# S5's output operands loaded ahead, a gate tile moved behind cross attention, and two moves at the feed-forward half's start and end

## The chip, the cores and the metric

The kernel runs on one NeuronCore of one Trainium2 chip. Its five engines each work through a queue of their own, in order: TensorE (PE, matrix products), VectorE (DVE), ScalarE (ACT), GpSimd (POOL), and SyncE (SP), which here issues the DMA transfers. The metric is the device time in microseconds (us); 0.2% of it is 3.3 us.

## The reference

One encoder layer, without masks, for two sequences of 512 tokens and 1024 channels, in float32, followed by a last RMS norm. The two sequences have weights in common, so the kernel handles them as one batch of 1024 columns.

```python
xn = rmsnorm(x, norm_mix);  mn = rmsnorm(mem, norm_mem)
u, q, k, v, xq, g = split(xn @ w_in)
y_s5   = z * sigmoid(z @ w_glu + b_glu)     # z = gelu(S5 scan both ways of u + d*u)
y_diff = differential attention of rope(q), rope(k), v
y_x    = cross attention of xq over 256 memory rows (mk, mv from mn @ w_mem_kv)
merged = sum over n of sigmoid(g[n]) * (branch[n] @ w_up[n])
x = x + merged @ w_out
gate, up = split(rmsnorm(x, norm_ffn) @ w_ffn_in)
x = x + (silu(gate) * up) @ w_ffn_out
y = rmsnorm(x, norm_final)
```

## The kernel before

**Products.** A float32 product is made of three: each operand is split into a rounded high part and the low rest (`split`: ACT casts the high part, L128, DVE subtracts for the low one, L129), and PE does high x high, low x high and high x low (L61). Tiles have 128 rows, 512 columns go through at a time; `xh, xl` are the halves of the normed input, `wh, wl` those of a weight tile, which arrives as `wf` (L140). A tile of `w_in` takes 48 such matmuls, 24 for each sequence.

**What sets the order.** The kernel's program is written in stages, and PE's order of work within a stage is mixed by hand: `queue` is a list of generators, `fill(n)` takes about n matmuls out of it, between the steps of the work that has waits. Gate tiles (`gate_units`: 48 matmuls, a tanh on ACT, a store to `gD` at L376) are what is mostly drawn on. The table `NG` says how many gate tiles each of three stages may use; its last number is for the stage from S5's output to the product with `w_glu`. Except where `PE.on` fixes PE's order, the framework orders the instructions of each engine by its own estimate of when they can start. Room in SBUF comes in named pools with a number of slots (`open_tags`); a new tile waits for the last user of the slot that it gets.

**S5's output (L1495 to L1524).** Convolution kernels of the 32 channel groups (`gD5`, in DRAM) and state outputs (`cD`) have been prepared. Four output groups follow, o = 0 to 3, each of 8 channel groups. A group loads `c_r` and `c_n` (L1502, L1503, 576 KB each) and its kernels `w_` in eight pieces (L1506), then PE does for each channel group three products, with `w_`, `c_r` and `c_n` in this order (L1517 to L1519), ACT copies the result to `y_` (L1520), and SP stores it in eight pieces (L1522). One tag `ow` with six slots holds all three operands of two groups, and the loads of a group are written behind the stores of the one before. Between the groups, PE does gate tiles.

**Cross attention.** 32 steps (4 heads, 2 sequences, 4 row blocks): scores, softmax, a `fill(5)`, two transposes of `e` (L64), the split of those into `xpTh`, `xpTl`, another `fill(5)`, and every four steps six matmuls with the memory's values (`bkoo`). The queue behind it ends with the first tile of the differential attention's queries, `units(w_in[4])`, whose result DVE turns with rope tables (L685, L687).

**The first feed-forward half.** `out_tile` makes x1 = x + merged @ w_out (L899 adds), 8 tiles of rows; the last four output tiles, for rows 3 and 7, are interleaved. `operands(i)` norms tiles i and i + 4, makes four sums of quadrants (`quad_sums`: DVE L907, L909, L910, POOL L908) and splits all seven operands into `th`, `tl`. The half's 22 weight tiles (KFF) each hold gate and up weights, 2 x 2 blocks; a Winograd scheme needs seven products for what plain blocks do in eight, 84 matmuls a tile. For it `weights4(i)` splits the blocks A11, A12, A22 and makes four sums S1 to S4 on POOL (L954 to L957, tile `ws`), which are split too, into the pool `aps`. DVE combines the products (L1035), norms (L1087), and makes the activation `ac` (L1090, L1091), with a tanh on ACT (L1088) and a product on POOL (L1089); `ac` goes to DRAM as `aD`. `rs` and `acc` are the norm's factors, for which PE does a few small products (`onec`, `ident`).

**Its end.** The second half needs the activations back in pairs: `act_pair(p)` loads `fa` and `fb` (L1054, L1055) and makes quad sums `ts`. The first two pairs are loaded and summed early, while the last tiles still run, and split (`pairs`) when the loop is done.

The tag `ld`, with four slots of 512 KB, is used by loads of many stages, `fa` and `fb` among them; `ws` had two slots of its own.

Of the kernel before, what the change touches and what calls it, by code (L numbers as in the profile page):

```python
# [37 lines left out]

NPREP = (16, 27)

NG = (7, 5, 7)
ROUND = 12582912.0


# [23 lines left out]
def encoder(ctx: ExitStack, tc: tile.TileContext, a, out):  # L68
# [547 lines left out]
    for _ in xq_units(0):  # L616
        pass
    xq = {h: xq_units(h) for h in range(1, 4)}
    queue += [xq[1], gate_units(), xq[2], xq[3], v_units(0, v0), units(a["w_in"][4], xh, xl, dq0.__setitem__)]
    PE.on = True  # L620
    steps = [(h, s, lt) for h in range(4) for s in range(NS) for lt in range(4)]
    es, pT = {}, {}
# [1 line left out]
    for i in range(-AHEAD, len(steps) + 1):  # L624
        if i + AHEAD < len(steps):
            h, s, lt = steps[i + AHEAD]
            if h and s == lt == 0:
                finish(xq[h])
            ms = slice(s * NMEM, (s + 1) * NMEM)
            qh, ql = (q_[:, lt * P : (lt + 1) * P] for q_ in qs[h, s])  # L630
            sc = bank("sc")
            PE.matmul(sc[:, :NMEM], qh, mkh[h][:, ms], start=True, stop=False)
            PE.matmul(sc[:, :NMEM], qh, mkl[h][:, ms], start=False, stop=False)
            PE.matmul(sc[:, :NMEM], ql, mkh[h][:, ms], start=False, stop=True)
            e, r = softmax_parts(xa, xcol, sc[:, :NMEM], NMEM, P ** -0.5, "x", bufs=3)
# [12 lines left out]
        fill(5)  # L648
        if i > 0 and steps[i - 1][2] == 3:
            h, s, _ = steps[i - 1]  # L650
            pTh, pTl = pT.pop((h, s))
            oo = bank("oo")
            hs = slice(h * P, (h + 1) * P)
            for j in range(2):
                PE.matmul(oo, mvh[s][:, j, hs], pTh[:, j, :], start=(j == 0), stop=False)
                PE.matmul(oo, mvh[s][:, j, hs], pTl[:, j, :], start=False, stop=False)
                PE.matmul(oo, mvl[s][:, j, hs], pTh[:, j, :], start=False, stop=(j == 1))
            osb = xa.tile([P, L], F32, tag="osb", name="xosb", bufs=1)
            S.copy(osb, oo)
            nc.sync.dma_start(bD[2, h, :, s * L : (s + 1) * L], osb)  # L660
        half_piece(last_e)
# [221 lines left out]
    ves.close()  # L883
    tes = ExitStack()
    open_tags(tes, side="right", th0=2, tl0=2)
    ses = ExitStack()
    open_tags(ses, side="right", x1=4, xr=2, ts=1)
    x1D = drp.tile([KD, P, NT], F32, name="x1D")
# [24 lines left out]
    def quad_room(i):  # L913
        j = i // 2 % 2
        return slot(f"th{j}", [P, 7, L], F32R, "th"), slot(f"tl{j}", [P, 7, L], F32R, "tl")

    def quad_split(i, xa_, xb_, t_):

        th, tl = quad_room(i)
        split(th[:, 0], tl[:, 0], xa_[:, 0:L])  # L920
        split(th[:, 1:3].rearrange("p a n -> p (a n)"), tl[:, 1:3].rearrange("p a n -> p (a n)"), xb_)
        split(th[:, 3:5], tl[:, 3:5], t_[:, 0:2])
        split(th[:, 5:7], tl[:, 5:7], t_[:, 2:4])
        return th, tl

    def operands(i):
# [8 lines left out]
    def weights4(i):  # L935

        nonlocal last_w
        a1, a2 = (wp.tile([P, DM], F32, tag="wf", name="wf") for _ in range(2))
        nc.sync.dma_start(a1, a["w_fg"][i])
        last_w = nc.sync.dma_start(a2, a["w_fu"][i])  # L940
        res = {}

        def sp(pool, src, sfx, *names):
            n = len(names) * H
            wh, wl = (pool.tile([P, DM], F32R, tag=t_ + sfx, name=t_, bufs=2) for t_ in ("wh", "wl"))
            split(wh[:, :n], wl[:, :n], src)
            for j, nm in enumerate(names):
                res[nm] = (wh[:, j * H : (j + 1) * H], wl[:, j * H : (j + 1) * H])

        sp(wp, a1, "", "A11", "A12")  # L950
        sp(wp, a2[:, H:], "", "A22")
        yield res
        s12, s34 = (slot("ws", name="ws") for _ in range(2))
        PO.tensor_tensor(out=s12[:, :H], in0=a2[:, :H], in1=a2[:, H:], op=ALU.add)  # L954
        PO.tensor_tensor(out=s12[:, H:], in0=s12[:, :H], in1=a1[:, :H], op=ALU.subtract)
        PO.tensor_tensor(out=s34[:, H:], in0=a1[:, H:], in1=s12[:, H:], op=ALU.subtract)
        PO.tensor_tensor(out=s34[:, :H], in0=a1[:, :H], in1=a2[:, :H], op=ALU.subtract)  # L957
        yield
        sp(aps, s12, "s", "S1", "S2")
        sp(aps, s34, "s", "S3", "S4")  # L960
        yield
# [96 lines left out]
    for i in range(KFF):  # L1058
        w = res0
        if i > 0:  # L1060
            wg = weights4(i)
            w = next(wg)
            next(wg)
            next(wg)
        if i == 1:
            prep = prepare(pes, pieces[NPREP[1] :])
            next(prep)
        elif i == KFF - 3:
            assert next(prep, None) is None
            pes.close()  # L1070
            open_tags(ses, side="right", ts=1)
            open_tags(fes, ts2=1)
        if i == KFF - 1:
            acts = [act_pair(0), act_pair(1, "ts2")]
            PE.on = True

        ps = products(i, w)
        p0 = next(ps)
        if i == 0:
            for s in range(NS):  # L1080
                _, bc = rstd(accs[s], DM)
                S.copy(accs[s], bc)
        gf0, gf1, up0, up1 = quadrants(ps, p0)
        ac = ap2.tile([P, NT], F32, tag="ac", name="ac")
        for s, gf, up in ((0, gf0, up0), (1, gf1, up1)):
            cs = slice(s * L, (s + 1) * L)
            V.tensor_tensor(out=gf, in0=gf, in1=accs[s], op=ALU.mult)  # L1087
            last_t = S.activation(out=ac[:, cs], in_=gf, func=AF.Tanh, scale=0.5)  # L1088
            PO.tensor_tensor(out=up, in0=up, in1=accs[s], op=ALU.mult)  # L1089
            V.scalar_tensor_tensor(out=ac[:, cs], in0=ac[:, cs], scalar=1.0, in1=gf, op0=ALU.add, op1=ALU.mult)  # L1090
            V.tensor_tensor(out=ac[:, cs], in0=ac[:, cs], in1=up, op=ALU.mult)  # L1091
        nc.sync.dma_start(aD[i], ac)
        if 1 <= i < KFF - 3:
            half_piece((last_t, last_sum))

    fes.close()
    open_tags(phase, yo=4)
    y2 = [slot("yo", [P, 2, NT], name=f"y{m}") for m in range(4)]  # L1100
    y = [y2[m // 2][:, m % 2] for m in range(KD)]
    pairs = [quad_split(i, *act) for i, act in enumerate(acts)]

# [154 lines left out]
def s5_gen(k):  # L1258
# [234 lines left out]
    yield  # L1493

    rt.close()  # L1495
    k.open_tags(rt, side="right", x2=2, ow=6, sy=2)
    yv = k.yD.rearrange("(g h) j s c -> j h g (s c)", h=16)
    for o in range(4):
# [3 lines left out]
        nc.sync.dma_start(c_r, cD[o, 0])  # L1502
        nc.sync.dma_start(c_n, cD[o, 1])  # L1503
        gv = gD[gs].rearrange("g h t q -> h g (t q)")
        for j in range(8):
            nc.sync.dma_start(w_[j * 16 : (j + 1) * 16], gv[:, :, (7 - j) * 16 : (7 - j) * 16 + 128])  # L1506
# [5 lines left out]
        for g4 in range(2):  # L1512
            ps = aux()
            for g in range(4):
# [3 lines left out]
                PE.matmul(d_, c_r[:, gg, 0:P], x2[:, 0, 2 * gg : 2 * gg + 2, :].rearrange("p s c -> p (s c)"), start=False, stop=False)  # L1518
                PE.matmul(d_, c_n[:, gg, 0:P], x2[:, 1, 2 * gg : 2 * gg + 2, :].rearrange("p s c -> p (s c)"), start=False, stop=True)  # L1519
            S.copy(y_[:, 4 * g4 : 4 * g4 + 4, :].rearrange("p g c -> p (g c)"), ps)  # L1520
        for j in range(8):
            nc.sync.dma_start(yv[j, :, gs], y_[j * 16 : (j + 1) * 16])  # L1522
    yield
# [97 lines left out]
```

## Time and profile before

| what | value |
|---|---|
| median of 3 runs | 1651.42 us (1650.65 to 1651.42) |
| the profiled execution's own time | 1648.71 us |
| its span in the profile | 1646.9 us |
| mean granted TensorE clock | 0.988 |
| PE busy | 1597.5 us, 97% |
| DVE, ACT, POOL busy | 1175.2, 633.5, 550.4 us |

The profile comes from one execution, and its span is 1.8 us shorter than that execution's time. The stages touched by the change lie in it at about 255 to 316 us (S5's output), 510 to 524 (end of cross attention), 957 to 1005 (start of the first feed-forward half) and 1345 to 1420 (its end). In a row of the timeline stand the start, the duration, engine, line and operation, and in brackets the idle time just before it with what ended it. A matmul's duration overlaps the next one's, so how fast PE goes is read from the distance of two starts.

### The profile page before, as it was taken

Reading aid. Unit: us, or ns where it says so; the run is one execution under the profiler, and the core shown is the slowest. Engines: PE = TensorE matmul, PEld = TensorE weight load, DVE = VectorE, ACT = ScalarE, POOL = GpSimd, SP = SyncE. Lnnn points to the kernel's source line nnn. Section 1 sums busy time; section 2 is a strip of 40 time slices with the busy share of each in tenths; the row PEclk is TensorE's granted clock in tenths of the full one; section 3 lists DMA queues with packets and bytes.
Section 4 is the critical chain, followed back from the end, with each engine's and each line's share of the span. In section 5 each row is a group of like instructions: output and inputs, shape, how many; then the busy total and the mean of one; then the engine's idle time right before and its main releaser. Section 6 shows DMA issues by size and latency. Waiting matters only on the chain.

```text
span 1646.9 us, 21707 instructions
## 1 busy us (share of the span) xinstructions
PE 1597.5 (97%) x7812; PEld 1317.8 (80%) x7812; DVE 1175.2 (71%) x1860; ACT 633.5 (38%) x1130; POOL 550.4 (33%) x444
## 2 busy tenths in 40 slices
PE   7999999899999999999989999999999999999997
PEld 5788788788897778777767886888888887888887
DVE  7957897154775676766576657898998888886545
ACT  6534323245554355564233433333233332331122
POOL 0001100000333221200555344666666665344242
PEclk9999999999999999999999998999999999999998
DMA  9354343737664110145785542433333322887632
GB/s 366 123 165 150 110 157 111 233 120 249 234 231 150 52 59 22 54 144 178 241 301 166 163 130 64 145 131 105 129 118 106 119 99 94 291 322 243 213 116 102
DMA packets 109355, 259.61 MB, mean 158 GB/s; under 512 B 14016, under 2 KB 42432, under 8 KB 109248
## 3 DMA queue, kind: packets, MB, share of 16 engines
q1 hardware_dynamic: 109248, 258.23, 46.1%
q8 instruction: 61, 1.00, 0.3%
q14 instruction: 46, 0.38, 0.1%
HBM read 174.85 MB, written 83.33 MB: 157 GB/s over the span
## 4 chain that ended last, share of the span: by engine, by line
PE 79%; DVE 10%; DMA 3%; issue 2%; POOL 2%; ACT 2%; SPq 1%; DVEq 0%; POOLq 0%; ACTq 0%
PE bkmm L61 68%; PE bktr L61 3%; PE bksc L61 2%; PE bkoo L61 2%; PE bktr L64 2%; DVE wl L129 2%; DVE st L1492 1%; PE bktr L1474 1%; POOL mg L726 1%; POOL up L1089 1%; DMA yt<-bD 1%; DVE hl L132 1%; DVE xt L243 0%; DMA wD<-hl 0%; DMA raw<-in_w_fo 0%
## 5 line engine op out<-in xcount | busy, mean ns | idle before, releaser
L61 PE MATMUL bkmm<-xh,wh 128*128 128x512 f32 x640 | 255.4, 399 | 1.2 <-ACT wh L128 1.2
L61 PE MATMUL bkmm<-xh,wl 128*128 128x512 f32 x640 | 250.9, 393 | 2.3 <-DVE wl L129 2.3
L61 PE MATMUL bkmm<-xl,wh 128*128 128x512 f32 x640 | 250.6, 392 | 0.0
L61 PE MATMUL bkmm<-tl,wh 128*128 128x512 f32 (+1 forms) x621 | 243.3, 392 | 3.3 <-DVE tl L129 3.3
L61 PE MATMUL bkmm<-th,wl 128*128 128x512 f32 (+1 forms) x621 | 241.5, 390 | 3.4 <-DVE wl L129 3.4
L61 PE MATMUL bkmm<-th,wh 128*128 128x512 f32 (+1 forms) x621 | 243.2, 392 | 0.0
L129 DVE TENSOR_TENSOR wl<-wf,wh 128x1024 fp32r<-128x1024 f32 (+1 forms) x133 | 152.0, 1143 | 71.8 <-ACT wh L128 63.4
L128 ACT CAST wh<-wf 128x1024 fp32r<-128x1024 f32 (+1 forms) x133 | 117.7, 885 | 204.2 <-PE bkmm L61 138.0
L424 POOL TENSOR_TENSOR raw<-raw 128x128 f32<-128x128 f32 x36 | 22.3, 620 | 400.3 <-DVE hl L132 396.9
L61 PEld LDWEIGHTS bkmm<-xh,wh 128*128 128x128 f32 x640 | 120.3, 188 | 32.0 <-issue 7.9
L61 PEld LDWEIGHTS bkmm<-xh,wl 128*128 128x128 f32 x640 | 120.2, 188 | 29.6 <-DVE wl L129 3.1
L61 PEld LDWEIGHTS bkmm<-tl,wh 128*128 128x128 f32 x621 | 117.7, 190 | 28.4 <-DVE tl L129 4.4
L61 PEld LDWEIGHTS bkmm<-th,wl 128*128 128x128 f32 x621 | 117.2, 189 | 27.7 <-DVE wl L129 3.9
L61 PE MATMUL bkmm<-th,w 128*128 128x512 f32 x432 | 139.2, 390 | 0.0
L61 PEld LDWEIGHTS bkmm<-xl,wh 128*128 128x128 f32 x640 | 120.4, 188 | 22.4 <-issue 0.4
L61 PEld LDWEIGHTS bkmm<-th,wh 128*128 128x128 f32 x621 | 117.6, 189 | 25.6 <-ACT wh L128 1.2
L1089 POOL TENSOR_TENSOR up<-up,acc 128x512 f32<-128x512 f32 x44 | 84.6, 1942 | 93.6 <-DVE up L1035 93.6
L61 PEld LDWEIGHTS bkmm<-th,w 128*128 128x128 f32 x432 | 81.1, 188 | 17.5 <-DVE up L1035 0.7
L132 DVE SCALAR_TENSOR_TENSOR hl<-raw,hl 128x384 fp32r<-128x384 f32 (+1 forms) x72 | 72.9, 1016 | 24.0 <-ACT hl L131 23.9
L487 ACT ACTIVATE e<-bksc,nb 128x512 f32<-128x512 f32 (+1 forms) x96 | 58.8, 615 | 70.0 <-DVE nb L482 51.7
L61 PE MATMUL bkmm<-tl,w 128*128 128x512 f32 x216 | 84.1, 389 | 0.0
L61 PE MATMUL bkmm<-yh,wh 128*128 128x512 f32 x192 | 78.0, 407 | 3.3 <-DVE gl L722 2.9
(628 smaller groups left out, 3524.7 us busy)
## 6 DMA issues: line engine op xcount, KB each, us to landing
wf<-in_w_in SPq DMA_DIRECT2D x40, 512.0 KB, 3.9
wD<-hl SPq DMA_DIRECT2D x36, 512.0 KB, 2.9
w<-wD SPq DMA_DIRECT2D x36, 512.0 KB, 4.5
wD<-hl SPq DMA_DIRECT2D x36, 384.0 KB, 2.9
w<-wD SPq DMA_DIRECT2D x36, 384.0 KB, 3.4
gD<-gt SPq DMA_DIRECT2D x24, 512.0 KB, 2.9
gl<-gD SPq DMA_DIRECT2D x24, 512.0 KB, 4.0
wf<-in_w_fg SPq DMA_DIRECT2D x22, 512.0 KB, 3.5
```

The costliest lines, as they stand in the source:

```text
L61: return self.put(self.eng.matmul(*args, **kw))
L64: return self.put(self.eng.transpose(*args, **kw))
L128: h = S.copy(hi, src)
L129: l_ = V.tensor_tensor(out=lo, in0=src, in1=hi.bitcast(F32), op=ALU.subtract)
L132: l_ = V.scalar_tensor_tensor(out=lo, in0=src, scalar=scale, in1=hi.bitcast(F32), op0=ALU.mult, op1=ALU.subtract)
L424: PO.tensor_tensor(out=a22, in0=a21, in1=a22, op=ALU.add)
L487: last_x = S.activation(out=e, in_=sc, func=AF.Exp, bias=nb, scale=scale, accum_out=sm)
L726: PO.tensor_tensor(out=mg[m], in0=mg[m], in1=gt, op=ALU.add)
L1089: PO.tensor_tensor(out=up, in0=up, in1=accs[s], op=ALU.mult)
L1474: PE.matmul(ps[:, g * P : (g + 1) * P], w_[:, gg * P : (gg + 1) * P], u_[:, 8 * o + gg, :], start=True, stop=True)
L1492: V.tensor_tensor(out=sv[:, :, :, i], in0=p_, in1=q_, op=ALU.add)
```

## The change

There are four parts.

**S5's output.** The tag `ow` is divided: `oc` with four slots for `c_r` and `c_n`, `ow` with three for the kernels. Both are loaded for groups 0 and 1 ahead of the loop; the kernels of group o + 2 are loaded at the start of group o's work, and its `c_r`, `c_n` after group o's matmuls, ahead of group o's stores. `NG` goes from (7, 5, 7) to (7, 5, 6).

**Cross attention.** The gate tile so freed is put in the queue ahead of `units(w_in[4])`, and the last step fills 15 instead of 5.

**Feed-forward start.** `ws` takes its two slots of a tile from `ld`; the pool `ffs` for the split sums is opened early, on the other side of memory; and the first weight tile's S1 to S4 are made and split ahead of `operands(2)` and `operands(3)`. The splits of later weight tiles yield to the last operand's split.

**Feed-forward end.** Since `ld` now also holds `ws`, `fa` and `fb` get their slots only behind the sums of the last tiles. `tsa` and `tsb` hold the quad sums, and the room of y's tiles is handed out in the order 0, 1, 3, 2.

```diff
-NG = (7, 5, 7)
+NG = (7, 5, 6)
-    queue += [xq[1], gate_units(), xq[2], xq[3], v_units(0, v0), units(a["w_in"][4], xh, xl, dq0.__setitem__)]
+    queue += [xq[1], gate_units(), xq[2], xq[3], v_units(0, v0), gate_units(), units(a["w_in"][4], xh, xl, dq0.__setitem__)]
-        fill(5)
+        fill(5 if i < len(steps) else 15)
+    aes = ExitStack()
+    aps = aes.enter_context(tc.tile_pool(name="ffs", bufs=1, side="right", reuse_waits="tile"))
-        split(th[:, 5:7], tl[:, 5:7], t_[:, 2:4])
+        last_q = split(th[:, 5:7], tl[:, 5:7], t_[:, 2:4])
-        s12, s34 = (slot("ws", name="ws") for _ in range(2))
+        s12, s34 = (slot("ld", name="ws") for _ in range(2))
-    ap2 = phase.enter_context(tc.tile_pool(name="ffn", bufs=1, reuse_waits="tile"))
-    fes = ExitStack()
-    open_tags(fes, ws=2)
     w0 = weights4(0)
     res0 = next(w0)
+    next(w0)
     next(w0)
     ops.append(operands(2))
     ops.append(operands(3))
     ses.close()
-    aps = fes.enter_context(tc.tile_pool(name="ffs", bufs=1, reuse_waits="tile"))
-    next(w0)
+    ap2 = phase.enter_context(tc.tile_pool(name="ffn", bufs=1, reuse_waits="tile"))
+    fes = ExitStack()
-            w = next(wg)
+            with yielding(last_q):
+                w = next(wg)
-            open_tags(ses, side="right", ts=1)
-            open_tags(fes, ts2=1)
+            open_tags(fes, side="right", tsa=1, tsb=1)
-            acts = [act_pair(0), act_pair(1, "ts2")]
+            acts = [act_pair(0, "tsa"), act_pair(1, "tsb")]
...
-    k.open_tags(rt, side="right", x2=2, ow=6, sy=2)
+    k.open_tags(rt, side="right", x2=2, oc=4, ow=3, sy=2)
...
+    def kernels_in(o):
+        w_ = slot("ow", [P, 8, P], name="w_")
...
+    def c_in(o):
+        c_r, c_n = (slot("oc", [P, 8, 144], name=n_) for n_ in ("c_r", "c_n"))
...
+    ins = []
+    for o in range(2):
+        c_ = c_in(o)
+        ins.append((kernels_in(o), *c_))
     for o in range(4):
         gs = slice(8 * o, 8 * o + 8)
-        c_r, c_n = (slot("ow", [P, 8, 144], name=n_) for n_ in ("c_r", "c_n"))
-        w_ = slot("ow", [P, 8, P], name="w_")
-        nc.sync.dma_start(c_r, cD[o, 0])
-        nc.sync.dma_start(c_n, cD[o, 1])
...
+        w_, c_r, c_n = ins[o]
+        if o < 2:
+            w2 = kernels_in(o + 2)
...
+        if o < 2:
+            ins.append((w2, *c_in(o + 2)))
         for j in range(8):
             nc.sync.dma_start(yv[j, :, gs], y_[j * 16 : (j + 1) * 16])
```

**Where instructions move.** SP's queue around S5's third group stood before as follows; `w__2734` are the kernels of group 2, `w__2787` those of group 3, `y__2642` and `y__2695` the results of groups 0 and 1.

```order
L1502 DMA c_r<-cD 128x1152
L1503 DMA c_n<-cD 128x1152
L1506 DMA w__2734<-gD_1052 16x8x128
L1522 DMA yD<-y__2642 16x8x128 x8
L1506 DMA w__2734<-gD_1052 16x8x128 x3
L1522 DMA yD<-y__2695 16x8x128 x8
L1506 DMA w__2734<-gD_1052 16x8x128 x4
L1502 DMA c_r<-cD 128x1152
```

It now stands as follows, with `w__2708` for group 3's kernels and `y__2667`, `y__2720` for the results of groups 0 and 1.

```order
L1509 DMA w__2708<-gD_1052 16x8x128
L1514 DMA c_r<-cD 128x1152
L1515 DMA c_n<-cD 128x1152
L1544 DMA yD<-y__2667 16x8x128 x8
L1509 DMA w__2708<-gD_1052 16x8x128 x7
L1514 DMA c_r<-cD 128x1152
L1515 DMA c_n<-cD 128x1152
L1544 DMA yD<-y__2720 16x8x128 x8
```

Group 2's kernels have gone from here to a much earlier place, ahead of the last of the kernels' stores to `gD5`; its c_r and c_n have kept theirs, behind one piece of group 3's kernels. On PE, groups 0 and 1 have no gate matmuls behind them any more: the last rows of group 1 are followed by group 2's (`w__2655`), and then by single gate matmuls among its rows.

```order
L1537 MATMUL bktr<-u__1194,w__2646 128x128
L1538 MATMUL bktr<-x_2717,c_r 128x128
L1539 MATMUL bktr<-x_2717,c_n 128x128
L1537 MATMUL bktr<-u__1194,w__2655 128x128
L1538 MATMUL bktr<-x_2761,c_r 128x128
L1537 MATMUL bktr<-u__1194,w__2655 128x128
L1538 MATMUL bktr<-x_2761,c_r 128x128
L61 MATMUL bkmm<-xh_123,wh 128x512
```

The 54 gate matmuls that stood before at the place of the fourth of these rows come among and behind groups 2 and 3.

On PE at the end of cross attention, the last transposes were followed by the output products:

```order
L64 MATMUL bktr<-ident,e 128x128 x2
L61 MATMUL bkoo<-xpTh,mkvh 128x512
L61 MATMUL bkoo<-xpTl,mkvh 128x512
L61 MATMUL bkoo<-xpTh,mkvl 128x512
L61 MATMUL bkoo<-xpTh,mkvh 128x512
```

Now 24 matmuls of a weight tile, the first half of `w_in[4]`, come between, of which the first stand here:

```order
L64 MATMUL bktr<-ident,e 128x128 x2
L61 MATMUL bkmm<-xh_123,wh 128x512
L61 MATMUL bkmm<-xl_131,wh 128x512
L61 MATMUL bkmm<-xh_123,wl 128x512
L61 MATMUL bkmm<-xh_124,wh 128x512
```

The six `bkoo` rows follow behind these 24, unchanged.

On POOL at the feed-forward start, before, behind the sums of the first weight tile:

```order
L956 TENSOR_TENSOR ws<-wf,ws 128x512
L176 TENSOR_TENSOR acc<-acc,nsq 128x512 x3
L908 TENSOR_TENSOR ts<-x_7_9185,x_3_9184 128x512
L954 TENSOR_TENSOR ws<-wf 128x512
L957 TENSOR_TENSOR ws<-wf 128x512
```

Now, with the new lines 959 to 962 for the sums and 910 for the operands' `ts`:

```order
L961 TENSOR_TENSOR ws<-wf,ws 128x512
L176 TENSOR_TENSOR acc<-acc,nsq 128x512 x2
L959 TENSOR_TENSOR ws<-wf 128x512
L962 TENSOR_TENSOR ws<-wf 128x512
L176 TENSOR_TENSOR acc<-acc,nsq 128x512
L960 TENSOR_TENSOR ws<-ws,wf 128x512
L910 TENSOR_TENSOR ts<-x_7_9192,x_3_9191 128x512
```

Three sums of the second weight tile (L959, L962, L960) have moved ahead of the operands' `ts`. On PE the S products over the first two operand pairs now come ahead of the first product that reads the third pair. On DVE, near the end of the loop, one row `ts<-fa` of the second act pair stands ahead of the last split of sums, and the three rows of the first pair a tile's length before it.

More of the change, by code (lines that the diff above doesn't have):

```diff
@@ L915, in quad_room @@
         return slot(f"th{j}", [P, 7, L], F32R, "th"), slot(f"tl{j}", [P, 7, L], F32R, "tl")
+    last_q = None
     def quad_split(i, xa_, xb_, t_):
+        nonlocal last_q
         th, tl = quad_room(i)
@@ L1098, in encoder @@
     fes.close()
+    aes.close()
+    open_tags(ses, side="right", ts=1)
     open_tags(phase, yo=4)
-    y2 = [slot("yo", [P, 2, NT], name=f"y{m}") for m in range(4)]
+    y2 = [slot("yo", [P, 2, NT], name=f"y{m}") for m in (0, 1, 3, 2)]
+    y2[2:] = y2[:1:-1]
     y = [y2[m // 2][:, m % 2] for m in range(KD)]
@@ L1495, in s5_gen @@
     rt.close()
-    k.open_tags(rt, side="right", x2=2, ow=6, sy=2)
+    k.open_tags(rt, side="right", x2=2, oc=4, ow=3, sy=2)
     yv = k.yD.rearrange("(g h) j s c -> j h g (s c)", h=16)
+    def kernels_in(o):
+        w_ = slot("ow", [P, 8, P], name="w_")
+        gv = gD[8 * o : 8 * o + 8].rearrange("g h t q -> h g (t q)")
+        for j in range(8):
+            nc.sync.dma_start(w_[j * 16 : (j + 1) * 16], gv[:, :, (7 - j) * 16 : (7 - j) * 16 + 128])
+        return w_
+    def c_in(o):
+        c_r, c_n = (slot("oc", [P, 8, 144], name=n_) for n_ in ("c_r", "c_n"))
+        nc.sync.dma_start(c_r, cD[o, 0])
+        nc.sync.dma_start(c_n, cD[o, 1])
+        return c_r, c_n
+    ins = []
+    for o in range(2):
+        c_ = c_in(o)
+        ins.append((kernels_in(o), *c_))
     for o in range(4):
         gs = slice(8 * o, 8 * o + 8)
-        c_r, c_n = (slot("ow", [P, 8, 144], name=n_) for n_ in ("c_r", "c_n"))
-        w_ = slot("ow", [P, 8, P], name="w_")
-        nc.sync.dma_start(c_r, cD[o, 0])
-        nc.sync.dma_start(c_n, cD[o, 1])
-        gv = gD[gs].rearrange("g h t q -> h g (t q)")
-        for j in range(8):
-            nc.sync.dma_start(w_[j * 16 : (j + 1) * 16], gv[:, :, (7 - j) * 16 : (7 - j) * 16 + 128])
+        w_, c_r, c_n = ins[o]
+        if o < 2:
+            w2 = kernels_in(o + 2)
         x2 = slot("x2", [P, 2, 8 * NS, NC], name="x2")
```

## The prediction

> **What bounds the kernel now.** I read the page first, for the engine that fills the span.
>
> ```profile
> span 1646.9 us, 21707 instructions
> PE 1597.5 (97%) x7812; PEld 1317.8 (80%) x7812; DVE 1175.2 (71%) x1860; ACT 633.5 (38%) x1130; POOL 550.4 (33%) x444
> ```
>
> TensorE (PE) is busy 97% of 1646.9 us. The change takes no matmul out, so all it can win is idle PE time, 1646.9 - 1597.5 = 49.4 us, and PE time at a reduced clock. Next, the view of waits, for PE alone, says who ended that idle time (total, times, longest).
>
> ```profile
> PE bkmm L61 <- DVE wl L129: 10.3, 9, 3.4
> ...
> PE bktr L1517 <- DMA w__2734<-gD: 3.6, 1, 3.6
> PE bkmm L61 <- DVE tl L129: 3.3, 2, 1.7
> ...
> PE bkoo L61 <- DVE xpTl L129: 2.0, 1, 2.0
> ```
>
> Each of the four edits stands at one of these rows: the kernels of S5's third group (3.6), the end of cross attention (2.0), the start of the first feed-forward half (tl, 3.3) and its end (the longest wl, 3.4). Third, busy time by windows, whose eighth figure is the granted PE clock; the columns ahead are the five engines' busy time.
>
> ```profile
> 300.00:305.00 5.00, 3.72 (x19) 3.75 (x20) 0.00 (x0) 0.00 (x0) 0.00 (x0) 0.66 1.01 289
> 988.70:1001.50 12.80, 8.85 (x23) 5.25 (x23) 12.14 (x13) 8.81 (x12) 3.28 (x3) 0.60 0.14 41
> 1345.00:1393.00 48.00, 48.00 (x213) 39.77 (x212) 43.25 (x49) 14.39 (x19) 29.94 (x18) 1.00 0.25 85
> 1393.00:1403.00 10.00, 6.55 (x23) 4.96 (x22) 5.18 (x8) 2.30 (x4) 0.89 (x1) 0.83 0.29 107
> ```
>
> The third row is the undisturbed loop: 213 matmuls in 48.00 us, 0.225 us each at full clock. The others are three of the four places: besides waiting, PE ran there at 0.66, 0.60 and 0.83 of its clock. So a stall is priced as its wait and the slow matmuls behind it.
>
> **Part 1, S5's output.** What PE did:
>
> ```profile
> 285.05 0.39 PE L1519 MATMUL bktr<-x,c_n 128*128 128x128 f32 x2
> 285.19 0.48 PE L61 MATMUL bkmm<-xh,wh 128*128 128x512 f32 x1
> ...
> 297.34 0.39 PE L61 MATMUL bkmm<-xh,wl 128*128 128x512 f32 x1
> 301.28 0.57 PE L1517 MATMUL bktr<-u__1194,w__2734 128*128 128x128 f32 x2 [3.55 <-DMA w__2734<-gD]
> ```
>
> Group 1 ends at 285.2, gate matmuls fill until 297.6, then PE waits until 301.3 for group 2's kernels: 3.7 us. Of the 3.72 us busy at 0.66 behind it, about a third, 1.3 us, is lost, and some 0.3 us past the window: 5.3 us together. The cause stands in SP's queue, and the DMA view of 277.5 to 284.2 gives the landing times (last column, us).
>
> ```profile
> 277.88 0.32 SPq L376 DMA_DIRECT2D gD<-gt  x1
> ...
> 280.55 2.66 SPq L140 DMA_DIRECT2D wf<-in_w_in  x1
> 283.31 0.38 SPq L1502 DMA_DIRECT2D c_r<-cD  x1
> ...
> 293.57 3.71 SPq L1522 DMA_DIRECT2D yD<-y__2695  x8
> 297.33 1.85 SPq L1506 DMA_DIRECT2D w__2734<-gD  x4
> ...
> c_r<-cD SPq DMA_DIRECT2D x1, 576.0 KB, 6.5
> c_n<-cD SPq DMA_DIRECT2D x1, 576.0 KB, 7.5
> ```
>
> The last four pieces of the kernels are issued behind group 1's eight stores, at 297.33. The change loads group 2's kernels long before, so this wait goes. What is late next is c_r. It still needs room that group 0 gives up, so it is issued where it was, at about 283.3 (283.7 with one kernel piece newly ahead of it), into the same backlog of gD and wf transfers, and lands 6.5 us later, at 289.8 to 290.2. PE now takes group 2 directly behind group 1, without the gate matmuls that stood between. Its second matmul reads c_r, so PE waits from about 285.6 to 290.0, 4.4 us. The nearest row for the slow clock behind that is the one above, 1.6 us. Nothing of group 3 comes late: its c_r, issued at about 295.4 and landing 4 to 6 us later, is needed only about 300 to 302, behind ten gate matmuls. New price 6.0, old 5.3: I take 0, with ends of -5.3 (no wait for c_r) and +2 (1.5 us later still). The gate tile that moves behind cross attention (48 matmuls, 48 x 0.225 = 10.8 us) is work in another place; six gate tiles are left to hide the way from S5's stores to the product with w_glu.
>
> **Part 2, cross attention's end.** PE first, then DVE:
>
> ```profile
> 519.26 0.50 PE L61 MATMUL bkoo<-xpTh,mkvh 128*128 128x512 f32 x1 [0.95 <-ACT xpTh L128]
> 521.80 0.50 PE L61 MATMUL bkoo<-xpTl,mkvh 128*128 128x512 f32 x1 [2.04 <-DVE xpTl L129]
> ...
> 518.96 1.23 DVE L129 TENSOR_TENSOR wl<-wf,wh 128x1024 fp32r<-128x1024 f32 x1 [1.41 <-ACT wh L128]
> ...
> 521.33 0.41 DVE L129 TENSOR_TENSOR xpTl<-bktr,xpTh 128x256 fp32r<-128x256 f32 x1
> ```
>
> The last transposes are followed at once by the six output matmuls, which wait 0.95 + 2.04 us; 3.0 us, and with the pipeline's refilling, 0.2 us each time, about 3.4. Now 24 matmuls of the next tile stand between, 24 x 0.225 = 5.4 us, more than the 3.4. The 24 were due right afterwards anyway, and their weights are there. Hidden behind those 5.4 us: ACT's copy and DVE's 0.41 us, with the 1.23 us split ahead of it. Gain 3.4; ends 2.0 (the split for the next tile comes later) and 3.4.
>
> **Part 3, the feed-forward start.** PE, then DVE and POOL:
>
> ```profile
> 988.79 0.48 PE L61 MATMUL bkmm<-th,wh 128*128 128x512 f32 x1
> ...
> 996.16 0.80 PE L61 MATMUL bkmm<-tl,wh 128*128 128x512 f32 x1 [1.66 <-DVE tl L129]
> ...
> 984.91 1.78 DVE L129 TENSOR_TENSOR tl<-x,th 128x512 fp32r<-128x512 f32 x1
> ...
> 987.36 0.65 DVE L907 TENSOR_TENSOR ts<-x 128x512 f32<-128x512 f32 x1
> ...
> 994.89 1.21 DVE L129 TENSOR_TENSOR tl<-ts,th 128x1024 fp32r<-128x1024 f32 x1
> ...
> 997.36 2.36 DVE L129 TENSOR_TENSOR wl<-ws,wh 128x1024 fp32r<-128x1024 f32 x2 [0.24 <-ACT wh L128]
> ...
> 984.56 1.58 POOL L176 TENSOR_TENSOR acc<-acc,nsq 128x512 f32<-128x512 f32 x1 [7.17 <-ACT rs L192]
> 987.43 1.72 POOL L908 TENSOR_TENSOR ts<-x,x 128x512 f32<-128x512 f32 x1 [1.29 <-DVE rs L193]
> ```
>
> The window 988.70 to 1001.50 holds 23 PE rows, by the view of groups 16 of them 128x512 matmuls and 7 small ones:
>
> ```profile
> L61 PE MATMUL bkmm<-tl,wh 128*128 128x512 f32 x7 | 4.4, 633 | 3.3 <-DVE tl L129 3.3
> ...
> L64 PE MATMUL bktr<-ident,rs 128*128 128x128 f32 x4 | 1.1, 434 | 0.7 <-DVE rs L193 0.7
> ```
>
> (count behind the x, mean ns ahead of the second bar; the wait behind it). At full clock that is 16 x 0.225 + 7 x 0.07 = 4.1 us; it took 12.8, so 8.7 are lost. PE has nothing else to do: all its products but those of the weights' sums (S1 to S4) wait for the last operands, the last ready at 994.89 + 1.21 = 996.1, and the sums' halves are split only at 997.4 to 999.7. The change moves those splits (2.36 us on DVE, and ACT's casts) beside the projection, where DVE and ACT wait for PE. Then the S products over the first two operand pairs, 24 x 0.225 = 5.4 us, come ahead of the last operands. Counted along the new order from 979.4, PE needs the last tl at about 996.2. DVE has three operations fewer ahead of it (two of the first gate tile, one weight split, 2.5 us by rows of 0.65 and 1.2 us), so it is ready at about 994 to 996. Two costs stand against it. GpSimd now makes the second tile's sums within this stretch, ahead of the operands' own ts: three more operations of some 1.7 us ahead of it on POOL's queue, and DVE slows beside POOL, as the 1.78 us split beside POOL's 984.56 shows against 0.65 for the same shape. And ACT changes its table twice more, behind the last cast. I leave 0.7 us of stall: gain 8.0, ends 4.0 and 8.7.
>
> [...]
>
> **Part 4, the feed-forward end.** DVE's last split of the weights' sums in three tiles, and PE:
>
> ```profile
> 1335.91 1.22 DVE L129 TENSOR_TENSOR wl<-ws,wh 128x1024 fp32r<-128x1024 f32 x1
> ...
> 1354.95 1.22 DVE L129 TENSOR_TENSOR wl<-ws,wh 128x1024 fp32r<-128x1024 f32 x1
> ...
> 1395.86 1.22 DVE L129 TENSOR_TENSOR wl<-ws,wh 128x1024 fp32r<-128x1024 f32 x1
> ...
> 1397.13 0.79 PE L61 MATMUL bkmm<-th,wl 128*128 128x512 f32 x1 [3.45 <-DVE wl L129]
> ```
>
> Undisturbed tiles are 1354.95 - 1335.91 = 19.04 us apart. The split two tiles on was due at 1393.05; it came 2.8 us late, because the sums of two act pairs (six DVE operations, some of them slowed by POOL) had pushed DVE back. The change loads both pairs later, into the sums' room, and puts pair 0's three operations and one of pair 1 ahead of that same split: four of 0.65 us, 2.6 us, two of them behind loads that themselves wait for the tile before. Less is inserted, but later, where DVE has less time to catch up: the split starts at about 1395.6 instead of 1395.9, a gain of 0.3, with the slow matmuls 0.5. Ends: 4 (on time: 3.45 and the slow matmuls behind it) and -3 (pair 1's load late). Behind it, pair 1's second load waits for the last split; its operands are first needed some 20 us on, which cover it.
>
> **Sum.** 0 - 3.4 - 8.0 - 0.5 = -11.9 us against the profiled execution's 1648.71 (span 1646.9 and 1.8 around it): 1636.8. The median of the runs shown, 1651.42, lies 2.7 above that execution, so 1639.5 in its terms.
>
> **Rivals.** (A) S5's wait goes altogether, since c_r lands earlier than I say: the DMA engines would have to drain the burst by 285.6. Against it stands the 6.5 us landing. It gives 1639.5 - 5.5 = 1634.
>
> (B) The feed-forward start becomes DVE's: in the window DVE was busy 12.14 of 12.80 us. If each of four more POOL operations costs it 1.1 us (1.78 - 0.65), the last tl comes at 994 + 4.4 = 998.4, 2.2 us late, and 1.6 us of slow clock follow as at S5: gain 8.0 - 3.8 = 4.2, time 1643.3. [...]
>
> (C) The feed-forward end gets worse: the load of pair 1 reaches DVE's queue late, and everything behind it, the last split first, waits. At 3.5 us later: 1643.
>
> (D) Slower: sums now live in the shared four-slot room, and POOL may make them at another time in each of the loop's 22 tiles. DVE is busy 43.25 of 48.00 us, 1.9 us free per tile; if the collision costs PE over 0.7 us a tile, 22 x 0.7 = 15 us outweigh the 11.9 by 3. At 0.8 us the time is 1657. Against it: PE's order from the third tile on is unchanged, and PE filled 48.00 of 48 us.
>
> (E) The slow clock near 990 does not come from the waits there and stays: only the waits return, 3.3 + 0.7 = 4.0 us by the view of groups. Gain 4.0 instead of 8.0, 1643.5. For it: no wait there is over 1.7 us. Against it: at S5 and at 1393 the clock fell only behind waits.
>
> **How the numbers follow.** 0.2% is 3.3 us, about what a measurement of this kernel can tell from no change. Forecast 0.58, A 0.12, B 0.12, C 0.07, D 0.06, E 0.05. Faster, below 1648.1: 0.56 + 0.12 + 0.10 + 0.04 + 0 + 0.04 = 0.86; same 0.08 (the bad ends of the forecast and of B, C and E); slower 0.06 (D). The range runs from 1632 (A with the good ends of parts 3 and 4) to 1648.5 (B or E with the bad ends of parts 1 and 4); it leaves out D and what lies beyond.
>
> **What would show it.** Right: a PE wait near 285 to 290 for c_r of group 2, none for w_ at 301; bkoo without waits; no tl wait over 1 us at the feed-forward start and clock 1.0 there; a wl wait of about 3 us kept at its end. Wrong: PE passing 290 without a wait (A), slow clock kept near 990 (B), a wait for fa or fb (C), or new gaps in every tile (D).

## The result, and the profile after

The changed kernel takes 1642.34 us (median of 4 runs, 1641.43 to 1642.99) against 1651.04 us before (median of 4, 1650.06 to 1651.42): ratio 0.9949, 95% interval [0.9937, 0.9961]. That is 8.7 us less, where 11.9 were forecast. The profiled execution took 1642.78 us; that of before, at 1648.71, lay 2.3 us under its own median, so the two traces differ by 5.9 us of span, two thirds of what the medians show.

The page's head and the view of waits for PE, of the changed kernel:

```profile
span 1641.0 us, 21700 instructions
PE 1594.0 (97%) x7812; PEld 1315.9 (80%) x7812; DVE 1176.3 (72%) x1860; ACT 635.9 (39%) x1132; POOL 551.3 (34%) x444
```

```profile
PE bkmm L61 <- DVE wl L129: 11.1, 8, 4.8
...
PE bktr L1538 <- DMA c_r<-cD: 5.7, 1, 5.7
...
PE bkmm L61 <- ACT th L128: 1.3, 1, 1.3
...
PE bkmm L61 <- DVE tl L129: 0.2, 1, 0.2
```

The bkoo rows are gone and the tl waits have shrunk from 3.3 to 0.2 us. In their place stand a wait of 5.7 us for c_r where 3.6 had been spent on w_, a new one of 1.3 us for th, and a longest wl wait of 4.8 where 3.4 had been. The windows of the same places (granted clock eighth):

```profile
280.00:300.00 20.00, 14.34 (x107) 13.69 (x107) 3.32 (x3) 6.41 (x8) 0.00 (x0) 0.83 0.78 223
984.90:996.20 11.30, 9.79 (x46) 7.81 (x45) 11.23 (x9) 3.44 (x4) 9.32 (x6) 1.00 0.02 3
988.70:1001.50 12.80, 11.29 (x55) 9.14 (x54) 12.73 (x12) 7.64 (x10) 5.52 (x3) 1.00 0.28 78
1380.00:1392.00 12.00, 7.17 (x29) 5.46 (x28) 10.69 (x15) 2.31 (x3) 3.88 (x2) 0.82 0.38 117
```

The feed-forward start runs at full clock now (it was 0.60), with 55 PE rows in the window that held 23. S5 (0.83) and the feed-forward end (0.82) still have a slow stretch.

One number for each place: PE time lost, added up over every matmul from the distance of its start to the next one's, less what that takes at full speed: 0.227 us for 128x512, the median distance in the loop of the profile before (1020 to 1340, clock 1.00), and 0.112 for 128x128, that of group 1 at S5 there (279 to 285).

| place | lost before | lost after | difference | forecast |
|---|---|---|---|---|
| S5's output | 8.0 | 9.4 | +1.4 | 0 |
| end of cross attention | 3.7 | 0.1 | -3.6 | -3.4 |
| feed-forward start | 9.1 | 2.1 | -7.0 | -8.0 |
| feed-forward end | 5.7 | 8.0 | +2.3 | -0.5 |

The four make -6.9; all other stretches together, where PE's order is the same, are about 1 us worse in this pair of executions. The table is of one execution each; what the other runs show of the same places stands below, behind the parts alone.

**S5.** SP's queue in the changed kernel (start, us, what is issued):

```profile
280.90 3.21 SPq L140 DMA_DIRECT2D wf<-in_w_in  x1
284.20 0.38 SPq L1509 DMA_DIRECT2D w__2708<-gD  x1
284.64 0.42 SPq L1514 DMA_DIRECT2D c_r<-cD  x1
```

The same load in the view of DMA issues (KB, median us to landing):

```profile
c_r<-cD SPq DMA_DIRECT2D x1, 576.0 KB, 6.9
```

And PE's timeline there:

```profile
285.61 0.39 PE L1537 MATMUL bktr<-u__1194,w__2655 128*128 128x128 f32 x2
291.66 0.77 PE L1538 MATMUL bktr<-x,c_r 128*128 128x128 f32 x2 [5.66 <-DMA c_r<-cD]
```

Group 2's kernels are there at once; its second matmul waits for c_r, as forecast. It was issued at 284.64 instead of 283.7 and took 6.9 us instead of 6.5, so the wait is 5.66 and not 4.4 us. Its room came free earlier: group 0's last product with c_r starts at 279.81. SP comes to the load 4.8 us later, and 3.21 of them it spends at one transfer ahead.

**Feed-forward end.** The load of the first pair in SP's queue, and DVE's timeline:

```profile
1371.02 0.43 SPq L1057 DMA_DIRECT2D fa<-aD  x1
...
1366.01 1.22 DVE L129 TENSOR_TENSOR wl<-ws,wh 128x1024 fp32r<-128x1024 f32 x1
...
1372.36 0.69 DVE L1038 TENSOR_TENSOR gf<-bkmm,p 128x512 f32<-128x512 f32 x1 [1.14 <-PE bkmm L61]
1375.80 0.69 DVE L909 TENSOR_TENSOR ts<-fa 128x512 f32<-128x512 f32 x1 [2.75 <-DMA fa<-aD]
...
1378.14 1.78 DVE L911 TENSOR_TENSOR ts<-fb,ts 128x512 f32<-128x512 f32 x1
...
1388.13 0.68 DVE L909 TENSOR_TENSOR ts<-fa 128x512 f32<-128x512 f32 x1
...
1389.33 1.22 DVE L129 TENSOR_TENSOR wl<-ws,wh 128x1024 fp32r<-128x1024 f32 x1
```

PE's, at the wait for that last split:

```profile
1390.60 0.79 PE L61 MATMUL bkmm<-th,wl 128*128 128x512 f32 x1 [4.83 <-DVE wl L129]
```

DVE reaches the first pair's sum at 1373.05 and stands until the load has landed, 2.75 us, with a tile's splits queued behind it. The last split of sums starts at 1389.33. The same split of the tile before started at 1366.01, so with tiles 19.04 us apart it was due at 1385.05: it is 4.3 us late, where it had been 2.8 before the change. PE, which has run to 1385.8, waits 4.83 us for it.

### The profile page after: what moved, and what is told of

The parts are those of the page before. It is cut to its first block, busy times and chain, and to the rows that moved or that the text cites. A ratio compares the mean times of both kernels' runs of the same rounds, so it can differ in the third digit from the quotient of the medians.

```text
span 1641.0 us, 21700 instructions
## 1 busy us (share of the span) xinstructions
PE 1594.0 (97%) x7812; PEld 1315.9 (80%) x7812; DVE 1176.3 (72%) x1860; ACT 635.9 (39%) x1132; POOL 551.3 (34%) x444
## 4 chain that ended last, share of the span: by engine, by line
PE 85%; DVE 6%; issue 3%; POOL 2%; DMA 2%; ACT 1%; SPq 0%; DVEq 0%; POOLq 0%; ACTq 0%
PE bkmm L61 74%; PE bktr L61 3%; PE bksc L61 2%; PE bkoo L61 2%; PE bktr L64 2%; PE bktr L1480 1%; DVE wl L129 1%; POOL mg L726 1%; PE bktr L1451 1%; DVE xt L243 0%; POOL up L1092 0%; DMA yt<-bD 0%; PE bktr L1419 0%; DMA c_r<-cD 0%; DVE tl L129 0%
## 5 line engine op out<-in xcount | busy, mean ns | idle before, releaser
L129 DVE TENSOR_TENSOR wl<-wf,wh 128x1024 fp32r<-128x1024 f32 (+1 forms) x133 | 148.1, 1113 | 86.9 <-ACT wh L128 77.7
```

What stands on the lines that cost most here:

```text
L129: l_ = V.tensor_tensor(out=lo, in0=src, in1=hi.bitcast(F32), op=ALU.subtract)
```

## The experiments

Each experiment was timed in five rounds beside the kernel before on the same chip, e9_no_pool in three.

**The parts alone.** e1_s5_only is the kernel before with the S5 part:

```diff
-    k.open_tags(rt, side="right", x2=2, ow=6, sy=2)
+    k.open_tags(rt, side="right", x2=2, oc=4, ow=3, sy=2)
...
+        if o < 2:
+            w2 = kernels_in(o + 2)
...
+            ins.append((w2, *c_in(o + 2)))
```

> The kernel before with the S5 part alone (rooms oc and ow, operands loaded ahead), without the gate tile's move. Theory: the wait for the kernels w_ is only exchanged for a wait for c_r of group 2 (5.7 us in the changed kernel, 3.6 before), so the time is that of before or up to 2 us more: 1651 to 1653. Rival (the loads ahead win the old wait, and the loss lies elsewhere): 3 to 5 us less, 1646 to 1648.

Measured: 1652.13 against 1650.23 us, ratio 1.0007, [0.9996, 1.0018]: no gain that can be told from nothing. In its view of waits the wait for w_ has gone and this row has come:

```profile
PE bktr L1532 <- DMA c_r<-cD: 5.1, 1, 5.1
```

The wait is exchanged, not removed; the rival falls.

e2_cross_only is the kernel before with the cross attention part:

```diff
-NG = (7, 5, 7)
+NG = (7, 5, 6)
...
-        fill(5)
+        fill(5 if i < len(steps) else 15)
```

and the gate tile in the queue. 

> The kernel before with the gate tile moved behind cross attention and the last fill of 15, nothing else. Theory: the two waits of the output products (0.95 and 2.04 us) go, nothing comes in their place: 3.4 us less, 1647.6, and no bkoo row in the view of waits. Rival (the wait comes back further on, at the differential attention's first scores): under 1 us less.

Measured: 1646.77 against 1650.23 us, ratio 0.9968, [0.9957, 0.9980], that is 5.3 us less with 3.3 to 7.1 as its interval (the two medians differ by 3.5). PE fills the window that had held the waits:

```profile
512.00:523.50 11.50, 11.50 (x52) 9.49 (x52) 3.43 (x7) 2.03 (x3) 2.58 (x2) 1.00 0.33 116
```

Before, the same window had 8.51 us of PE and 39 matmul records. Nothing came back further on: the view of waits holds no bkoo row, and PE's next idle time over 0.15 us is one of 1.05 us at 752 us, which the profile of before has as well, with 1.01.

e3_ffn_only is the changed kernel with these two parts undone:

```diff
-    k.open_tags(rt, side="right", x2=2, oc=4, ow=3, sy=2)
+    k.open_tags(rt, side="right", x2=2, ow=6, sy=2)
-        fill(5 if i < len(steps) else 15)
+        fill(5)
```

and NG, the queue and S5's loop as before. 

> The kernel before with both feed-forward moves, without the S5 and cross attention parts. Theory: 7 us won at the start, 2.3 lost at the end, 4.8 less in all: 1646.2, with a wl wait of about 4.8 us near the loop's end. Rival (slow clock near the start is independent of its waits): 2 us less at most.

Measured: 1645.42 against 1650.23 us, ratio 0.9966, [0.9953, 0.9980], 5.6 us less. Its waits are those of before's order at S5, with one more of 2.1 us for group 3's kernels (`w__2787`), and those of after in the feed-forward half:

```profile
PE bkmm L61 <- DVE wl L129: 11.2, 9, 4.8
...
PE bktr L1523 <- DMA w__2734<-gD: 3.0, 1, 3.0
```

The three ratios, 1.0007, 0.9968 and 0.9966, multiply to 0.9941, within the interval of the whole.

**The places over all runs.** Each run has most of the four places in one of the two orders, so the measure of the table above can be taken from every trace (PE time lost, us; taken anew for the two kernels themselves, it comes within 0.2 us of that table). e5 to e9, which follow below, are left out at the places that they alter further.

| place | with the order of before | with the order of after | mean difference | forecast |
|---|---|---|---|---|
| S5's output | before 8.0, e2 8.7, e3 8.8 | after 9.4, e1 8.9, e6 9.1, e7 8.8, e9 9.0 | +0.5 | 0 |
| end of cross attention | before 3.7, e1 5.3, e3 5.4 | all others 0.0 to 0.1 | -4.8 | -3.4 |
| feed-forward start | before 9.1, e1 9.6, e2 9.0 | after 2.0, e3 2.0, e5 2.1, e6 2.0 | -7.2 | -8.0 |
| feed-forward end | before 5.6, e1 5.5, e2 5.6 | after 7.8, e3 6.8, e5 8.8, e7 7.7, e9 7.0 | +2.1 | -0.5 |

The sum is -9.4. It is near the 8.7 us of the medians, whose interval is 6.4 to 10.4. The pair of profiled executions shows less because that of before lost less than e2 and e3 at S5's output, and less than e1 and e3 at the end of cross attention, in the same order. What differs at the second place is plain in the traces. In before, e1 and e3 PE stands in the same two waits, 0.95 and 2.04 us. Behind them it goes on at full clock in before, but in e1 and e3 its clock falls for some 3 us (to 0.64 in the window of e1 below), and they lose 5.3 and 5.4 us there against 3.7. The windows of before and e1:

```profile
524.00:528.00 4.00, 4.00 (x19) 3.34 (x18) 2.04 (x4) 0.63 (x1) 1.08 (x2) 1.00 0.17 66
...
524.00:528.00 4.00, 4.00 (x13) 3.11 (x12) 2.04 (x4) 1.11 (x2) 1.07 (x2) 0.64 0.18 70
```

**S5's new wait.** e5_gates_between sets a gate tile between the groups whose operands are there and the two others:

```diff
     with behind():
         next(s5)
+    gates(1)
+    with behind():
+        next(s5)
     next(s5, None)
...
-    gates(NG[2])
+    gates(NG[2] - 1)
...
+        if o == 1:
+            yield
```

> The changed kernel with one gate tile (48 matmuls, 10.9 us) set between S5's groups 0, 1 and groups 2, 3, and one less behind. Theory: c_r of group 2 lands at about 291.5, the gate tile covers PE until about 296, so the wait of 5.7 us and the 1.8 us of slow clock behind it go: 6 to 7.5 us less than the changed kernel, about 1635.5. Rival (S5's results come later and the product with w_glu waits for them): a new wait near 368, gain under 2 us.

Measured: 1635.58 against 1651.71 us, ratio 0.9898, [0.9884, 0.9911], 0.51% better than the change's 0.9949, some 8 us. PE is full through the place of the wait, at full clock:

```profile
284.00:300.00 16.00, 16.00 (x96) 14.10 (x95) 2.45 (x2) 4.95 (x6) 0.00 (x0) 1.00 0.82 240
```

So the wait and the slow clock behind it were a matter of PE's order: the gate tile keeps PE busy from 285.39 to 296.38, and c_n, issued between 284 and 286, landed 7.7 us later, by 293.7. With it, S5's part gains what it could not alone: by the measure of the tables PE loses 1.6 us there, against 8.0 to 8.8 with the order of before. No wait for S5's results appeared in front of the product with w_glu, so that rival falls too.

**The act pairs.** e6_sums_after queues DVE's sums of the first two pairs behind the last split:

```diff
-            acts = [act_pair(0, "tsa"), act_pair(1, "tsb")]
+            acts = [act_load(0), act_load(1)]
...
+    with yielding(last_sp):
+        acts = [(*act, quad_sums(*act, tag)) for act, tag in zip(acts, ("tsa", "tsb"))]
```

> The changed kernel with DVE's sums of the first two act pairs queued behind the last split of the weights' sums (their loads and room unchanged). Theory: DVE's wait for fa (2.75 us) and the four sums ahead of the last split cause PE's wait of 4.8 us there; without them it is at most 1 us and the slow clock behind it goes: 5 to 7 us less than the changed kernel, about 1636. [...] Rival 2 (the sums are then late for the second half): a new wait of 2 us or more behind 1400, nothing gained.

Measured: 1636.68 against 1650.23 us, ratio 0.9906, [0.9891, 0.9921], 0.43% better than the change, some 7 us. The wait at that place:

```profile
1383.93 0.50 PE L61 MATMUL bkmm<-th,wl 128*128 128x512 f32 x1 [0.62 <-DVE wl L129]
```

0.62 us instead of 4.83, at full clock. The sums moved behind the split, and one of them still stands 1.14 us for a load there, without a wait of PE's:

```profile
1388.63 0.69 DVE L911 TENSOR_TENSOR ts<-fb,ts 128x512 f32<-128x512 f32 x1 [1.14 <-DMA fb<-aD]
```

The last split starts at 1382.65, 19.04 us behind that of the tile before, so it is no longer late. POOL's order is unchanged and the wait went all the same, so POOL's products were not what set the split's time. Nor are the sums late for the second half, so rival 2 falls: behind 1400 PE has no wait over 0.3 us but the two of the last norm, 2.3 us for nsq and 0.7 for rs, which before has as well (2.3 and 0.6).

**What was left at the feed-forward start.** In the changed kernel four of DVE's operations there take 1.9 to 2.6 times what they take in e9, below, where POOL's sums are gone. DVE's timeline:

```profile
985.67 1.78 DVE L935 TENSOR_SCALAR x<-x,vec 128x1024 f32<-128x1024 f32 x1
...
987.45 1.70 DVE L909 TENSOR_TENSOR ts<-x 128x512 f32<-128x512 f32 x1
989.18 1.67 DVE L911 TENSOR_TENSOR ts<-x,ts 128x512 f32<-128x512 f32 x1
990.77 2.31 DVE L129 TENSOR_TENSOR tl<-x,th 128x1024 fp32r<-128x1024 f32 x1
993.00 1.77 DVE L912 TENSOR_TENSOR ts<-x,ts 128x512 f32<-128x512 f32 x1
994.70 2.47 DVE L129 TENSOR_TENSOR tl<-ts,th 128x1024 fp32r<-128x1024 f32 x2
```

POOL's, over the same time:

```profile
986.85 1.74 POOL L176 TENSOR_TENSOR acc<-acc,nsq 128x512 f32<-128x512 f32 x1
988.56 1.74 POOL L960 TENSOR_TENSOR ws<-ws,wf 128x512 f32<-128x512 f32 x1
990.25 1.74 POOL L910 TENSOR_TENSOR ts<-x,x 128x512 f32<-128x512 f32 x1
991.95 2.27 POOL L961 TENSOR_TENSOR ws<-wf,ws 128x512 f32<-128x512 f32 x1
```

ACT's:

```profile
994.86 1.04 ACT L128 CAST th<-ts 128x1024 fp32r<-128x1024 f32 x1 [2.93 <-DVE ts L912]
```

And PE's:

```profile
995.96 0.50 PE L61 MATMUL bkmm<-th,wh 128*128 128x512 f32 x1 [1.30 <-ACT th L128]
```

POOL works without a break, DVE behind it is late with its last sum (L912), ACT's cast of that sum waits 2.93 us for it, and PE 1.30 us for the cast.

e7_sums_behind queues GpSimd's sums of the second weight tile behind its ts. The author estimated that the two waits, 1.30 and 0.20 us, come from those sums beside DVE and would go, for 1.5 us less than the changed kernel, 1640.8:

```diff
+            if i == 1:
+                with tc.issue_after(last_po.ins):
+                    next(wg)
```

> The changed kernel with GpSimd's sums of the second weight tile queued behind its operand sum ts of the last pair. [...]

Measured: 1640.97 against 1651.71 us, ratio 0.9941, [0.9928, 0.9955], not to be told from the change's 0.9949. The estimate's ground falls, for PE still waits, 0.6 and 0.8 us for tl. The sums now run beside the last splits (L963 and L964, from 990.07 to 994.04), and DVE is slowed there instead:

```profile
990.58 4.54 DVE L129 TENSOR_TENSOR tl<-ts,th 128x1024 fp32r<-128x1024 f32 x2
```

These two splits took 2.47 us in the changed kernel, where POOL's sums had ended before them. From the norm's start to the last split's end DVE needs 995.12 - 983.61 = 11.51 us, as in the changed kernel (11.50). So not the place of ts in POOL's queue counts here, but that POOL works at all while DVE is the last. e9_no_pool takes POOL's work away:

```diff
+        if i == 1:
+            for d_, s_ in ((s12, a1), (s34, a2)):
+                S.copy(d_, s_)
+        else:
```

> The changed kernel without GpSimd's four sums for the second weight tile (ScalarE copies two weight tiles into their place instead, so that tile's S products are those of other numbers). Theory (DVE is slowed beside POOL, and this is what is left of the stall at the feed-forward start): DVE's operations between the last operand's norm and its last split take 0.7 and 1.2 us again instead of 1.7 and 2.3, except beside POOL's one ts; the last split ends 4 us or more earlier, the waits of 1.3 and 0.2 us go; the time is 1 to 2 us under the changed kernel's 1642.3. Rival (DVE's operations are long for another reason, their operands' place): their times stay, and so do the waits.

Measured: 1639.53 against 1652.42 us, ratio 0.9927, [0.9904, 0.9950], an interval that overlaps the change's: the time alone decides nothing. The trace does. There is no PE wait between 980 and 998, and PE is busy through the whole window:

```profile
984.90:996.20 11.30, 11.30 (x58) 9.47 (x57) 11.12 (x13) 7.36 (x10) 2.62 (x2) 1.00 0.17 46
```

DVE's timeline in e9:

```profile
986.25 0.74 DVE L935 TENSOR_SCALAR x<-x,vec 128x1024 f32<-128x1024 f32 x1
...
987.00 0.65 DVE L909 TENSOR_TENSOR ts<-x 128x512 f32<-128x512 f32 x1
987.69 1.67 DVE L911 TENSOR_TENSOR ts<-x,ts 128x512 f32<-128x512 f32 x1
989.28 1.21 DVE L129 TENSOR_TENSOR tl<-x,th 128x1024 fp32r<-128x1024 f32 x1
990.42 0.68 DVE L912 TENSOR_TENSOR ts<-x,ts 128x512 f32<-128x512 f32 x1
991.02 2.48 DVE L129 TENSOR_TENSOR tl<-ts,th 128x1024 fp32r<-128x1024 f32 x2
```

From the norm's start to the last split's end DVE needs 993.50 - 986.25 = 7.25 us, against 997.17 - 985.67 = 11.50 with POOL's sums, 4.25 more. It is four operations that differ: x 0.74 against 1.78 us, ts (L909) 0.65 against 1.70, the split behind them 1.21 against 2.31 and ts (L912) 0.68 against 1.77, 1.04 to 1.10 us each. The sum L911 takes 1.67 in both, since POOL still makes its own ts beside it in e9.

**All three.** e8_three joins e5, e6 and e7. 

> The changed kernel with all three: a gate tile between S5's groups, the act pairs' sums behind the last split, the second tile's sums behind ts. Theory: the gains add, 6.5 + 6 + 1.5 = 14 us less than the changed kernel, about 1628.5. Rival (some of the stalls share a cause or come back further on): less than 10 us.

Measured: 1629.21 against 1651.71 us, ratio 0.9864, [0.9851, 0.9878]. Against the change's 0.9949 that is 0.85%, 14 us, as was expected, though that sum counted 1.5 us for e7, which alone gave nothing; e5 and e6 gave the rest, some 8 and 7. The PE time lost is that of e5 at S5 (1.6 us) and 2.1 us at the feed-forward end, so the two gains stand side by side. This kernel is faster than both others; its span in the profile is 1627.4 us.

## Why the prediction was right, step by step

**The whole.** The sign was right, and 8.7 us less came for 11.9 forecast. The sizes were not all right: against the means over all runs part 1 was off by +0.5, part 2 by -1.4, part 3 by +0.8 and part 4 by +2.6. That part 2 gave more than forecast made up for half of what part 4 was off by, and that is luck. Nor does the time alone choose among the theories: 1642.34 lies 2.8 us above the forecast's 1639.5, and nearer to the prices of rivals B, C and E (1643.3, 1643, 1643.5). The traces choose.

**Part 1: mechanism right.** That the old wait would go and one for c_r come in its place is shown by e1 and by the row of 5.66 us. The forecast took c_r's landing time from before and let SP issue it at 283.7. SP stood 3.21 us at the transfer ahead, and the landing took 0.4 us longer. The prediction's own prices, 6.0 new and 5.3 old, made +0.7, which it took as 0; the pair of traces shows +1.4, the means over all runs +0.5, and e1 alone +1.2 with an interval of -0.7 to +3.0. Rival A, that the wait would go altogether, did not happen; e5 shows what it would have been worth with one gate tile in the right place, 6.4 to 7.2 us against the order of before, where the rival had put 5.5.

**Part 2: mechanism right, size too small.** 3.4 were forecast, 3.6 came in the pair of traces, 5.3 with an interval down to 3.3 in e2. No wait took its place. Besides the waits the forecast had put 0.2 us for each; by the starts of before, from 517.92 to 522.13, PE lost 3.5 us with 2.99 of waits, 0.27 more for each. The forecast priced the waits by an execution in which no slow clock followed them; in e1 and e3 one did, and the part was worth 5.3 and 5.4 us.

**Part 3: right, with a part of rival B.** When the waits went, the clock rose from 0.60 to 1.00; that settles rival E. Rival B put the cost at 4.4 us of DVE beside POOL and had PE wait 2.2 us for it, with 1.6 us of slow clock behind. e9 measured 4.25 us of DVE. PE lost 2.1 us in the changed kernel and 0.1 us in e9, so B's wait came, and its slow clock did not. The forecast had left 0.7 us for it, though it named POOL's sums as a cost. Most of PE's wait was for a cast on ACT, behind the slowed DVE sum (1.30 us), and only 0.20 us for tl. ACT's two table loads came behind that cast, at 999.31 and 1001.25, 1.28 us each, and PE waited for neither.

**Part 4: the step that failed.** "Less is inserted, but later ... the split starts at about 1395.6 instead of 1395.9, a gain of 0.3" counted the four sums at 0.65 us and named their loads as a danger only for pair 1. It was pair 0's load that counted: it is issued behind the store of the tile before, at 1371.02 by SP, and landed 4.75 us later, so DVE stood 2.75 us; one sum was slowed to 1.78 us beside POOL. The split came 4.3 us late instead of the 2.5 forecast. The term was -0.5 and measured +2.3 in the pair of traces and +2.1 over all runs, near the end that the forecast had set at +3. It is rival C's price with its mechanism at the other pair, and the wait for fa that the prediction named as a sign of C did come, on DVE. e6 shows the cause: with the sums behind the split PE's wait falls to 0.62 us.

**Rival D** did not happen: in the loop PE is busy 320.00 of 320 us, from 1020 to 1340, as it was before.

**The range.** Its ends do not follow from the terms given for them. A with the good ends of parts 3 and 4 makes 1634 - 0.7 - 3.5 = 1629.8, not 1632, and B or E with the bad ends of parts 1 and 4 makes 1648.8 or 1649.0, not 1648.5. The measured time lies well inside either way.

**Left open.** The slow stretch at 988 to 1001 before the change (0.60, with no wait over 1.66 us) went when the waits went, but the runs do not show what in the waits decides. The end of cross attention shows that it is not the waits alone: the same two waits, 0.95 and 2.04 us, were followed by a slow clock in e1 (0.64) and e3, and not in before (1.00). Why the feed-forward end loses 6.8 us in one run and 8.8 in another, with one and the same order, is open as well.

## What to carry to other kernels

When operands are loaded earlier, look at which of a step's operands is then last: here kernels came early and the state outputs, whose load stood behind other transfers in SP's queue, took over the wait, 5.66 us for 3.55. Look at what an engine does ahead of urgent work, and at the loads that this waits for: here DVE stood 2.75 us for a load of the act pairs, and the last split came 4.3 us late, while with the same sums behind the split (e6) it came on time and PE's wait fell from 4.83 to 0.62 us. And where independent work is at hand, try its place in the order of the bound engine: here one gate tile, 10.99 us in e5, set between the groups gave some 8 us, where the loads alone (e1) gave nothing that can be told from zero.

## What the runs showed of the hardware

Beside POOL, some of DVE's operations took longer in these traces and others did not. In the profile before, with POOL at work from 1382.76 to 1386.4, DVE's two operations with one operand in PSUM (`bkmm`) keep their 0.67 and 0.68 us, and a split with both operands in SBUF takes 2.31 us instead of 1.22. An operation with both operands in SBUF that starts together with a sum of POOL's, at 1384.58, keeps its 0.69 us; there POOL's sum takes 1.84 us, where one beside an operation with a PSUM operand takes 1.30 (at 1371.85 in the changed kernel):

```profile
1383.28 0.68 DVE L1035 TENSOR_TENSOR u<-bkmm,p 128x512 f32<-128x512 f32 x1
...
1384.58 0.69 DVE L1087 TENSOR_TENSOR gf<-gf,acc 128x512 f32<-128x512 f32 x1
1385.19 2.31 DVE L129 TENSOR_TENSOR wl<-wf,wh 128x1024 fp32r<-128x1024 f32 x1
```

Counted over the profile before, 122 operations of this shape (two tensors of 128x512 in, float32 out) with one in PSUM, and with POOL at work for over half of their time, took 0.67 to 0.69 us. Of 57 with both in SBUF the median was 1.65 us; 13 of them kept 0.65 to 0.69 us, and the other 44 took 0.80 to 1.79. The 77 with both in SBUF and POOL at work for less than half of their time took 0.68 to 0.73. The norm's scaling, with a single tensor in SBUF, took longer as well, 1.78 us in the changed kernel with POOL's sums beside it against 0.74 in e9. What in an operation decides is not shown. e9 gives the price here, 1.04 to 1.10 us for each of the four DVE operations that met POOL's sums.

How late a transfer landed depended here more on what was issued ahead of it than on its size: 64 KB took 2.3 us or 6.5, and 576 KB 5.6 or 6.9. From the view of DMA issues of the changed kernel, 270 to 300 us (KB each, median us to landing):

```profile
wf<-in_w_in SPq DMA_DIRECT2D x2, 512.0 KB, 7.3
w__2708<-gD SPq DMA_DIRECT2D x8, 64.0 KB, 2.2
yD<-y__2667 SPq DMA_DIRECT2D x8, 64.0 KB, 5.7
```

The stores of y and the pieces of w__2708 are of one size, and each of the two tiles shows both times. Of the stores, the six issued from 285.58 to 290, behind the backlog, took 6.5 us (median), and the last two 2.3. Of the pieces, the first, issued at 284.20, took 4.5 us, and the seven issued from 293.31 on 2.2. For 576 KB the time was 6.9 us at 284.64 and 5.6 at 296.68.
